# HGRN scores in one product for two heads: each query traded to the other head's tile, the second head read back by a transpose

## The chip, the cores and the metric

The kernel runs on one core of a Trainium2 chip. The metric is the device time of one execution in microseconds (us), as the median of three runs. A profile of one further execution gives the trace that is read here. The engines are called TensorE (PE in the rows; PEld is its loading of stationary operands), VectorE (DVE), ScalarE (ACT), GpSimd (POOL) and SyncE (SP, which issues most transfers).

## What is computed

A trunk of two layers over 256 positions of width 2048, in float32. Layer 0 mixes positions with a gated recurrence (HGRN2, 16 heads of width 128, chunks of 64), layer 1 with a gMLP; each is followed by a squared-ReLU MLP of width 8192. The change lies in the scores of the recurrence alone:

```
b = jnp.cumsum(g_t, axis=2)                                  # log decay, inside a chunk
rel = b[:, :, :, None, :] - b[:, :, None, :, :]
decay = jnp.exp(jnp.where(causal[:, :, None], rel, -jnp.inf))
scores = jnp.einsum('bhtd,bhtsd,bhsd->bhts', q_t, decay, k_t)
o = o_inter + jnp.einsum('bhts,bhse->bhte', scores, v_t)
```

The decay depends on query, key and feature, so the scores are no plain product. The kernel splits the causal triangle of 128 positions into levels. At the level with half-blocks of `h` positions, queries in the second half of a block of `2h` meet keys in its first half; both are scaled by their decay to the boundary between them, and a plain product over features gives the scores of that level. The levels are `h` = 32, 16, 8, the blocks of 8 on the diagonal (scaled to a point inside them), and `h` = 64 (between the two chunks of a 128 block).

## The kernel before

Weights come from HBM in tiles of 1 MB (`raw`, three buffers). Each is split in two: ScalarE casts it to a rounded part (line 127) and VectorE subtracts that for the rest (line 128), so that every projection is a few fast products of rounded operands (lines 158, 160 and 169 to 171). The split tiles `wt` are in a pool of five; a cast has to wait until TensorE has used the tile whose place it takes.

The recurrence runs over eight pairs of heads (`hp`, the loop of line 311). For each pair four projections are made: forget gates, queries, values (for two pairs at once, in even `hp`), gates. Tiles such as `k`, `q`, `dl` and `gl` are 128 features x 2 heads x 256 positions. For `h` = 32, 16, 8, VectorE makes exponents (lines 363, 364), ScalarE their exponential (365), and VectorE multiplies by key in the first halves and by query in the second halves of one tile `gl` (line 370). `kd`, `qd` are the operands of the diagonal blocks, `g64` that of level 64, and `gx` that of the scores between the two blocks of 128.

Line 411 then makes, for each of the five levels, four 128x128 products: two heads times two blocks of 128. In `gl` keys and queries lie side by side, so each product gives keys by queries of one head in the wanted corner, and useless numbers elsewhere. Line 413 copies the wanted places from PSUM into `Pm` under a mask (COPY_PREDICATED), for both heads and blocks in one instruction of 512 columns. Lines 433 and 434 multiply `Pm` by the values into `po`; lines 436 to 442 square and sum that into `pn`; the closure `norm` of line 451 is run in the next pair and fills `S2[hp]` (`s_7` in the rows for the last pair), which the out-projection needs.

These score products, and transposes, take plain float32 operands; the trace has two MATMUL records for such a product (line 411: 5 levels x 4 products x 8 pairs = 160 products, 320 records) and one for a transpose.

The order of instructions on each engine is made by a scheduler that places them on a timeline of its own; `high_priority` and `issue_after` in the code move a few of them. Each engine takes its instructions strictly in that order. Small products share four PSUM banks in turn (`bank`).

Of the kernel before, what the change touches and what calls it, by code (L numbers as in the profile page):

```python
# [8 lines left out]
F32 = mybir.dt.float32  # L9
FR = mybir.dt.float32r  # L10
U8 = mybir.dt.uint8
AF = mybir.ActivationFunctionType
ALU = mybir.AluOpType
PSUM = bass.MemoryType.PSUM

P = 128
T = 256
# [16 lines left out]
def trunk(ctx: ExitStack, tc: tile.TileContext, x, norm_mix, norm_mlp, final_norm, hgrn_w_in, hgrn_w_out,  # L34
# [3 lines left out]
    V, S, G, M = nc.vector, nc.scalar, nc.gpsimd, nc.tensor  # L38

    cp = ctx.enter_context(tc.tile_pool(name="cp", bufs=1))  # L40
# [160 lines left out]
                                       op0=ALU.mult, op1=ALU.subtract)  # L201


    masks = cp.tile([P, 5, P], U8, name="masks")
    rows0 = cp.tile([32, P], F32, name="rows0")
    rows = cp.tile([81, P], F32, name="rows")
    cols0 = cp.tile([P, 32], F32, name="cols0")
# [11 lines left out]
    with tc.tile_pool(name="x0", bufs=1) as x0, tc.tile_pool(name="x1", bufs=2) as x1:  # L219
        xt = [ht[:, :, c * 512:(c + 1) * 512] for c in range(4)]  # L220
        ssp = x0.tile([P, 2, 4], F32, name="ssp")
        nc.scalar.dma_start(out=rows0, in_=norm_mix.rearrange("l (k p) -> (l k) p", p=P))
        raws = [[raw_tile(0, 0), raw_tile(0, 1)],
                [raw_tile(1, 0), x0.tile([P, 8, 256], F32, name="raw1_1")]]
        for c in range(4):
            for h in range(2 if c == 0 else 1):
                w = 256 if c == 0 else 512
                nc.sync.dma_start(out=xt[c][:, :, h * w:(h + 1) * w],
                                  in_=x[0, :, c * 512 + h * w:c * 512 + (h + 1) * w].rearrange("(a p) d -> p a d", p=P))
                if c == 0:  # L230
                    load_part(0, raws[0][0], 2 * h, 2 * h + 2)
            for n in range(2):
                if n or c:
                    load_part(n, raws[n][c // 2], 4 * c, 4 * c + 4)
        pw = [psw.tile([P, 2, 512], F32, tag="pw", name=f"pw{n}") for n in range(2)]
        pc = bank("pc0")
        M.transpose(pc[:, 0:32], rows0, ident[0:32, 0:32])
        V.tensor_copy(cols0, pc[:, 0:32])
        for c in range(4):
            to_features(c, cols0)  # L240
            for n in range(2):
                split_weights(n, raws[n][c // 2], c, parts=1 if c or n else 2)
                mm_feat(pw[n], ready[n], S1, range(4 * c, 4 * c + 4))
        state["load"] = state["use"] = 2
        nc.sync.dma_start(out=rows[0:32, :], in_=norm_mlp.rearrange("l (k p) -> (l k) p", p=P))
        nc.sync.dma_start(out=rows[32:80, :], in_=hgrn_lb_logits.rearrange("l (k p) -> (l k) p", p=P))
        nc.sync.dma_start(out=rows[80:81, :], in_=hgrn_g_norm)
        mf32 = x0.tile([P, 5, P], F32, name="mf32")
        nc.sync.dma_start(out=mf32, in_=level_masks.rearrange("l p t -> p l t"))
        G.tensor_copy(masks, mf32)  # L250
        pc = bank("pc")
        M.transpose(pc[:, 0:81], rows, ident[0:81, 0:81])
        V.tensor_copy(cols, pc[:, 0:81])
        for c in range(4):
            for j in range(2):
                junk = x1.tile([P, 512], F32, tag="junk", name=f"junk{c}{j}")
                if j:
                    V.scalar_tensor_tensor(junk, xt[c][:, j, :], 1.0, xt[c][:, j, :], op0=ALU.mult, op1=ALU.mult,
                                           accum_out=ssp[:, j, c:c + 1])
                else:  # L260
                    S.activation(junk, xt[c][:, j, :], AF.Square, accum_out=ssp[:, j, c:c + 1])
        s2 = x0.tile([P, 2, 2], F32, name="s2")
        V.tensor_tensor(s2, ssp[:, :, 0:2], ssp[:, :, 2:4], op=ALU.add)
        ms = x0.tile([P, 2], F32, name="ms")
        V.tensor_tensor(ms, s2[:, :, 0], s2[:, :, 1], op=ALU.add)
        V.tensor_scalar(ms, ms, 1.0 / D, EPS, op0=ALU.mult, op1=ALU.add)
        G.tensor_tensor(r0c, ms, mhalf[:, 0:2], op=ALU.pow)
# [29 lines left out]
    with tc.tile_pool(name="hg", bufs=1) as hg, tc.tile_pool(name="hg2", bufs=2) as hg2:  # L297
# [1 line left out]
        G.memset(reset, 1.0)  # L299
        G.memset(reset[:, :, 0:1], 0.0)  # L300
        Pm = [hg.tile([P, 2, 3, P], F32, name=f"Pm{i}") for i in range(2)]
        for t in Pm:
            G.memset(t, 0.0)

        def wide(pool, tag, name):
# [2 lines left out]
        def flat(t):  # L308
            return t.rearrange("p a t -> p (a t)")

        for hp in range(NP):
# [41 lines left out]
            V.scalar_tensor_tensor(flat(q), flat(thq), 1.0, flat(zq), op0=ALU.add, op1=ALU.mult)  # L353


            Gs = []
            for h in (32, 16, 8):
                dl = wide(hg2, "dl", f"{hp}_{h}")
# [6 lines left out]
                S.activation(dl, dl, AF.Exp)  # L365
                gl = wide(hg2, "gl", f"{hp}_{h}")
                gv = flat(gl).rearrange("p (b j i) -> p b j i", j=2, i=h)
                for j, src in ((0, k), (1, q)):
                    sv = flat(src).rearrange("p (b j i) -> p b j i", j=2, i=h)
                    V.tensor_tensor(gv[:, :, j, :], dv[:, :, j, :], sv[:, :, j, :], op=ALU.mult)  # L370
                Gs.append((gl, gl))
            dd = wide(hg2, "dl", f"{hp}_d")
            cv = flat(c).rearrange("p (b i) -> p b i", i=8)
            V.tensor_tensor(flat(dd).rearrange("p (b i) -> p b i", i=8), cv,
# [4 lines left out]
            S.activation(kd, dd, AF.Exp, scale=-1.0)  # L379
            V.tensor_tensor(qd, qd, q, op=ALU.mult)  # L380
            V.tensor_tensor(kd, kd, k, op=ALU.mult)
            Gs.append((kd, qd))
            de = wide(hg2, "dl", f"{hp}_e")
            c8 = flat(c).rearrange("p (b i) -> p b i", i=64)
            V.tensor_tensor(flat(de).rearrange("p (b i) -> p b i", i=64), c8[:, :, 63:64].to_broadcast([P, 8, 64]),
# [6 lines left out]
            def ch(t):  # L392
                return t.rearrange("p a (m i) -> p a m i", i=64)

            g64 = wide(hg, "g64", hp)
            V.tensor_tensor(ch(g64)[:, :, 0::2, :], ch(ek)[:, :, 0::2, :], ch(k)[:, :, 0::2, :], op=ALU.mult)
            V.tensor_tensor(ch(g64)[:, :, 1::2, :], ch(eq)[:, :, 1::2, :], ch(q)[:, :, 1::2, :], op=ALU.mult)
            Gs.append((g64, g64))
            gx = wide(hg, "gx", hp)
            V.tensor_tensor(ch(gx)[:, :, 0::3, :], ch(g64)[:, :, 0::3, :],  # L400
                            ch(eq)[:, :, 1:3, 63:64].to_broadcast([P, 2, 2, 64]), op=ALU.mult)
            V.tensor_tensor(ch(gx)[:, :, 1, :], ch(ek)[:, :, 1, :], ch(k)[:, :, 1, :], op=ALU.mult)
            V.tensor_tensor(ch(gx)[:, :, 2, :], ch(eq)[:, :, 2, :], ch(q)[:, :, 2, :], op=ALU.mult)

            pm = Pm[hp % 2]
            for li, (kl, ql) in enumerate(Gs):
                sc = bank(f"sc{hp}_{li}")
                scv = sc.rearrange("p (a b t) -> p a b t", a=2, b=2)
                for j in range(2):
                    for b in range(2):  # L410
                        M.matmul(scv[:, j, b, :], lhsT=kl[:, j, b * P:(b + 1) * P], rhs=ql[:, j, b * P:(b + 1) * P],  # L411
                                 start=True, stop=True)
                V.copy_predicated(pm[:, :, 0::2, :],  # L413
                                  masks[:, li:li + 1, :].unsqueeze(1).to_broadcast([P, 2, 2, P]), scv)
            sx = bank(f"sx{hp}")
            sxv = sx.rearrange("p (a t) -> p a t", a=4)
            for j in range(2):
# [105 lines left out]
    st = Stats("c")  # L523
# [160 lines left out]
def _level_masks():  # L684
    import numpy as np

    s = np.arange(P)[:, None]
    t = np.arange(P)[None, :]
    m = [(s // (2 * h) == t // (2 * h)) & (s % (2 * h) < h) & (t % (2 * h) >= h) for h in (32, 16, 8)]
    m.append((s // 8 == t // 8) & (s <= t))  # L690
    m.append((s < 64) & (t >= 64))
    return np.stack(m).astype(np.float32)


# [19 lines left out]
```

## Time and profile before

| | before |
|---|---|
| median of 3 runs (lowest to highest) | 2217.31 us (2216.74 to 2219.0) |
| the profiled execution | 2219.78 us |
| its span, first to last instruction | 2218.0 us |
| TensorE busy | 2205.0 us, 99% |
| VectorE busy | 1343.0 us, 61% |
| ScalarE busy | 1047.8 us, 47% |
| granted TensorE clock, mean | 0.999 |

A time of the trace is compared with the profiled execution's own span; 1.78 us of that execution lie outside it. The recurrence takes about the first 470 us. In a timeline a row gives the start, the duration, the engine and line, and `x16` for sixteen records merged in one row. Matmuls are pipelined: a row's duration includes the tail that overlaps the next one, so the cost of a product on TensorE is read from start to start. The same holds for VectorE, where an instruction starts shortly before the listed end of the one ahead.

### The profile page before, as it was taken

How to read it: one execution, taken by the hardware profiler on the slowest of the kernel's cores; microseconds unless marked ns; L12 is line 12 of the kernel's file. 1: busy time of each engine (PE TensorE's matmuls, PEld its weight loads, DVE VectorE, ACT ScalarE, POOL GpSimd, SP SyncE). 2: the span in 40 equal slices, each digit the busy share in tenths (PEclk: the TensorE clock that was granted, in tenths of full speed). 3: DMA queues.
4: the chain of work that ended last, by engine and by line, in shares of the span. 5: the costliest groups of instructions: out<-in, count | busy, mean ns of one | idle time of the engine just before them, and what ended most of it. 6: DMA issues, size and time to landing. Idle time of an engine off the chain costs nothing.

```text
span 2218.0 us, 27973 instructions
## 1 busy us (share of the span) xinstructions
PE 2205.0 (99%) x11512; PEld 1894.9 (85%) x11512; DVE 1343.0 (61%) x1593; ACT 1047.8 (47%) x1293; POOL 10.2 (0%) x23
## 2 busy tenths in 40 slices
PE   9999999999999999999999999999999999999998
PEld 7888888888888888888888888888888888888887
DVE  7787877756555555555555558656555545554554
ACT  6666566555434433443444544444434433443443
POOL 0000000000000000000000000000000000000000
PEclk9999999999999999999999999999999999999999
DMA  7555555556556556655655657656566556556653
GB/s 239 166 171 168 157 171 153 191 179 188 192 190 195 193 190 193 191 178 192 202 194 187 205 171 215 206 184 195 185 200 191 193 176 206 191 191 189 191 181 123
DMA packets 309761, 414.28 MB, mean 187 GB/s; under 512 B 6801, under 2 KB 210818, under 8 KB 309378
## 3 DMA queue, kind: packets, MB, share of 16 engines
q1 hardware_dynamic: 309010, 411.44, 58.1%
q8 instruction: 90, 1.47, 0.3%
q10 hardware_dynamic: 624, 1.07, 0.1%
q14 instruction: 37, 0.30, 0.0%
HBM read 410.38 MB, written 2.10 MB: 186 GB/s over the span
## 4 chain that ended last, share of the span: by engine, by line
PE 99%; DMA 0%; issue 0%; ACT 0%; SPq 0%; DVE 0%; POOLq 0%; POOL 0%; ACTq 0%
PE pw L158 32%; PE pw L160 17%; PE pw L169 15%; PE pw L171 15%; PE pw L170 15%; PE sc L411 2%; PE xT L195 1%; DMA raw<-in_hgrn_w_in 0%; PE mix L599 0%; PE po L433 0%; PE pw L640 0%; PE pw L638 0%; PE pw L639 0%; PE pn L442 0%; PE sx L418 0%
## 5 line engine op out<-in xcount | busy, mean ns | idle before, releaser
L128 DVE TENSOR_TENSOR wt<-raw,wt 128x1024 fp32r<-128x1024 f32 (+1 forms) x769 | 923.5, 1220 | 758.1 <-ACT wt L127 757.8
L127 ACT CAST wt<-raw 128x1024 fp32r<-128x1024 f32 (+1 forms) x769 | 789.5, 1049 | 892.1 <-PE pw L171 458.4
L158 PE MATMUL pw<-s,wt 128*128 128x512 f32 x3072 | 733.5, 393 | 3.8 <-ACT wt L127 2.4
L158 PEld LDWEIGHTS pw<-s,wt 128*128 128x128 f32 x3072 | 568.9, 189 | 118.9 <-ACT wt L127 3.1
L169 PE MATMUL pw<-wt,s 128*128 128x512 f32 x1504 | 587.5, 391 | 0.0
L171 PE MATMUL pw<-wt,s 128*128 128x512 f32 x1504 | 587.0, 390 | 0.0
L170 PE MATMUL pw<-wt,s 128*128 128x512 f32 x1504 | 586.5, 390 | 0.0
L160 PEld LDWEIGHTS pw<-s,wt 128*128 128x128 f32 x3072 | 386.3, 191 | 10.9
L160 PE MATMUL pw<-s,wt 128*128 128x256 f32 x3072 | 391.4, 283 | 0.0
L171 PEld LDWEIGHTS pw<-wt,s 128*128 128x128 f32 x1504 | 282.3, 188 | 59.3
L170 PEld LDWEIGHTS pw<-wt,s 128*128 128x128 f32 x1504 | 282.4, 188 | 58.8
L169 PEld LDWEIGHTS pw<-wt,s 128*128 128x128 f32 x1504 | 282.4, 188 | 58.6 <-DVE z_f L179 0.2
L185 ACT CAST s<-a 128x512 fp32r<-128x512 f32 x64 | 39.6, 619 | 136.0 <-DVE a L518 136.0
L186 DVE TENSOR_TENSOR s<-a,s 128x512 fp32r<-128x512 f32 x64 | 44.3, 692 | 37.1 <-ACT s L185 37.1
L518 DVE SCALAR_TENSOR_TENSOR a<-z_ff 128x512 f32<-128x512 f32 x64 | 43.9, 685 | 0.3
L179 DVE TENSOR_TENSOR z_ff<-pw,tb_ff 128x512 f32<-128x512 f32 x64 | 43.8, 684 | 0.0
L178 ACT COPY tb_ff<-pw 128x512 f32<-128x512 f32 x64 | 37.2, 582 | 0.0
L199 ACT ACTIVATE s<-xT,cols 128x256 fp32r<-128x256 f32 x64 | 27.7, 473 | 19.3 <-PE xT L195 12.1
L200 DVE SCALAR_TENSOR_TENSOR s<-xT,cols,s 128x256 fp32r<-128x256 f32 x64 | 28.4, 479 | 8.8 <-ACT s L199 8.6
L413 DVE COPY_PREDICATED Pm<-masks,sc 128x512 f32<-128x512 uint8 x40 | 29.4, 734 | 1.2
L497 DVE SCALAR_TENSOR_TENSOR ht<-pw,col_c,ht 128x512 f32<-128x512 f32 x32 | 22.5, 746 | 5.3 <-PE pw L171 5.3
L411 PEld LDWEIGHTS sc<-gl 128*128 128x128 f32 x192 | 23.5, 191 | 0.8
(189 smaller groups left out, 733.4 us busy)
## 6 DMA issues: line engine op xcount, KB each, us to landing
raw<-in_mlp_w SPq DMA_DIRECT2D x256, 1024.0 KB, 5.7
raw<-in_hgrn_w_in SPq DMA_DIRECT2D x60, 1024.0 KB, 5.8
raw<-in_gmlp_w_in SPq DMA_DIRECT2D x32, 1024.0 KB, 5.6
raw<-in_hgrn_w_out SPq DMA_DIRECT2D x16, 1024.0 KB, 5.1
raw<-in_gmlp_w_out SPq DMA_DIRECT2D x16, 1024.0 KB, 5.1
raw<-in_hgrn_w_in SPq DMA_DIRECT2D x7, 512.0 KB, 9.5
ht<-in_x SPq DMA_DIRECT2D x3, 512.0 KB, 8.7
gb<-in_gmlp_ln_gain SPq DMA_DIRECT2D x8, 128.0 KB, 4.9
```

The source lines that it names most:

```text
L127: S.copy(wt[:, kk, 0:width], src[:, kk, :])
L128: V.tensor_tensor(wt[:, kk, width:2 * width], src[:, kk, :], f32(wt[:, kk, 0:width]), op=ALU.subtract)
L158: M.matmul(pt[:, n, :], lhsT=wt[:, n * P:(n + 1) * P], rhs=xk, start=(k == 0), stop=False)
L160: M.matmul(pt[:, n, 256:512], lhsT=wt[:, 256 + n * P:256 + (n + 1) * P], rhs=xk[:, 0:256], start=False, stop=(k == KT - 1))
L169: M.matmul(pt[:, n, :], lhsT=hi, rhs=wt[:, 0:512], start=(k == 0), stop=False)
L170: M.matmul(pt[:, n, :], lhsT=hi, rhs=wt[:, 512:1024], start=False, stop=False)
L171: M.matmul(pt[:, n, :], lhsT=lo, rhs=wt[:, 0:512], start=False, stop=(k == KT - 1))
L179: V.tensor_tensor(dst, pt[:, :, 0:256], tb, op=ALU.add)
L185: S.copy(dst[:, :, 0:256], src)
L186: V.tensor_tensor(dst[:, :, 256:512], src, f32(dst[:, :, 0:256]), op=ALU.subtract)
L411: M.matmul(scv[:, j, b, :], lhsT=kl[:, j, b * P:(b + 1) * P], rhs=ql[:, j, b * P:(b + 1) * P], start=True, stop=True)
L518: V.scalar_tensor_tensor(a.rearrange("p a t -> p (a t)"), z.rearrange("p a t -> p (a t)"), 0.0, z.rearrange("p a t -> p (a t)"), op0=ALU.m ...
```

## The change

Queries trade heads. In `gl` and `g64`, head 0's tile keeps its own keys but gets the queries of head 1, and the other way round. One product of tile 0 (stationary) by tile 1 (moving) then has, where the row is a key place and the column a query place, the scores of head 0, and where the row is a query place and the column a key place, the scores of head 1, transposed. So levels 32, 16, 8 and 64 take two products (one for each block of 128) and not four. Their result goes through a new tile `Px` under masks of both corners, in copies of 256 columns. What lies above the diagonal blocks in `Px` is copied to head 0's part of `Pm` under a sixth mask; TensorE transposes `Px` (two transposes into bank `st`), and VectorE copies the same places of that to head 1's part. The diagonal level keeps its four products (`sd`).

For each pair this makes 12 score products and 2 transposes of what was 20 products. On VectorE, multiplications by queries become two smaller ones (one for each head), the part of `gx` that reads `g64` becomes three, and five masked copies of 512 columns become one of 512 and six of 256: 24 instructions for 16. The masks are 6 x 128 columns for 5 x 128, their transfer 384 KB for 320 KB.

```diff
-                for j, src in ((0, k), (1, q)):
-                    sv = flat(src).rearrange("p (b j i) -> p b j i", j=2, i=h)
-                    V.tensor_tensor(gv[:, :, j, :], dv[:, :, j, :], sv[:, :, j, :], op=ALU.mult)
-                Gs.append((gl, gl))
+                kv = flat(k).rearrange("p (b j i) -> p b j i", j=2, i=h)
+                V.tensor_tensor(gv[:, :, 0, :], dv[:, :, 0, :], kv[:, :, 0, :], op=ALU.mult)
+                for a in range(2):
+                    V.tensor_tensor(second(gl[:, 1 - a, :], h), second(dl[:, a, :], h), second(q[:, a, :], h), op=ALU.mult)
+                Gs.append(gl)
...
-            V.tensor_tensor(ch(g64)[:, :, 1::2, :], ch(eq)[:, :, 1::2, :], ch(q)[:, :, 1::2, :], op=ALU.mult)
-            Gs.append((g64, g64))
+            for a in range(2):
+                V.tensor_tensor(ch(g64)[:, 1 - a, 1::2, :], ch(eq)[:, a, 1::2, :], ch(q)[:, a, 1::2, :], op=ALU.mult)
+            Gs.append(g64)
             gx = wide(hg, "gx", hp)
-            V.tensor_tensor(ch(gx)[:, :, 0::3, :], ch(g64)[:, :, 0::3, :],
-                            ch(eq)[:, :, 1:3, 63:64].to_broadcast([P, 2, 2, 64]), op=ALU.mult)
+            V.tensor_tensor(ch(gx)[:, :, 0, :], ch(g64)[:, :, 0, :],
+                            ch(eq)[:, :, 1, 63:64].to_broadcast([P, 2, 64]), op=ALU.mult)
+            for a in range(2):
+                V.tensor_scalar(ch(gx)[:, a, 3, :], ch(g64)[:, 1 - a, 3, :], ch(eq)[:, a, 2, 63:64], None, op0=ALU.mult)
...
-            for li, (kl, ql) in enumerate(Gs):
+            px = Px[hp % 2]
+            for li, gl in zip((0, 1, 2, 4), Gs):
                 sc = bank(f"sc{hp}_{li}")
-                scv = sc.rearrange("p (a b t) -> p a b t", a=2, b=2)
-                for j in range(2):
-                    for b in range(2):
-                        M.matmul(scv[:, j, b, :], lhsT=kl[:, j, b * P:(b + 1) * P], rhs=ql[:, j, b * P:(b + 1) * P],
-                                 start=True, stop=True)
-                V.copy_predicated(pm[:, :, 0::2, :],
-                                  masks[:, li:li + 1, :].unsqueeze(1).to_broadcast([P, 2, 2, P]), scv)
+                for b in range(2):
+                    M.matmul(sc[:, b * P:(b + 1) * P], lhsT=gl[:, 0, b * P:(b + 1) * P], rhs=gl[:, 1, b * P:(b + 1) * P],
+                             start=True, stop=True)
+                V.copy_predicated(px, masks[:, li:li + 1, :].to_broadcast([P, 2, P]),
+                                  sc[:, 0:T].rearrange("p (b t) -> p b t", b=2))
+            sc = bank(f"sd{hp}")
+            scv = sc.rearrange("p (a b t) -> p a b t", a=2, b=2)
+            for j in range(2):
+                for b in range(2):
+                    M.matmul(scv[:, j, b, :], lhsT=kd[:, j, b * P:(b + 1) * P], rhs=qd[:, j, b * P:(b + 1) * P],
+                             start=True, stop=True)
+            V.copy_predicated(pm[:, :, 0::2, :], masks[:, 3:4, :].unsqueeze(1).to_broadcast([P, 2, 2, P]), scv)
+            apart = masks[:, 5:6, :].to_broadcast([P, 2, P])
+            V.copy_predicated(pm[:, 0, 0::2, :], apart, px)
+            st = bank(f"st{hp}")
+            for b in range(2):
+                M.transpose(st[:, b * P:(b + 1) * P], px[:, b, :], ident)
+            V.copy_predicated(pm[:, 1, 0::2, :], apart, st[:, 0:T].rearrange("p (b t) -> p b t", b=2))
```

Three places show how the order moves. In these rows a name ends in a number of its own; the lines of the changed kernel are 418 (score products), 426 (diagonal products), 433 (transposes), 438 (`sx`) and 453, 454 (`po`), and 420, 428, 430, 434 (masked copies). The first place is TensorE in the first pair, from the score products to `po`; before:

```order
162 L411 MATMUL sc_2_567<-gl_8_531 128x128 x4
163 L411 MATMUL sc_3_573<-qd_536,kd_537 128x128 x4
164 L411 MATMUL sc_4_579<-g_0_548 128x128 x4
165 L418 MATMUL sx_585<-gx_551 128x128 x2
166 L158 MATMUL pw_734<-s_2_91,wt_1_594 128x512 x2
167 L158 MATMUL pw_734<-s_3_92,wt_1_594 128x512 x4
168 L160 MATMUL pw_734<-s_0_89,wt_0_591 128x256 x4
169 L160 MATMUL pw_734<-s_1_90,wt_0_591 128x256 x4
170 L160 MATMUL pw_734<-s_2_91,wt_1_594 128x256 x4
171 L160 MATMUL pw_734<-s_3_92,wt_1_594 128x256 x3
172 L433 MATMUL po_705<-Pm_439,v_702 128x256
```

The same stretch of TensorE in the changed kernel, in two parts, the first from level 64 to the transposes:

```order
167 L418 MATMUL sc_4_577<-g_0_555 128x128 x2
168 L426 MATMUL sd_581<-qd_543,kd_544 128x128 x4
169 L160 MATMUL pw_741<-s_1_90,wt_0_598 128x256 x3
170 L160 MATMUL pw_741<-s_2_91,wt_1_601 128x256 x4
171 L160 MATMUL pw_741<-s_3_92,wt_1_601 128x256 x4
172 L158 MATMUL pw_741<-s_4_93,wt_2_606 128x512 x4
173 L158 MATMUL pw_741<-s_5_94,wt_2_606 128x512
174 L433 MATMUL st_588<-ident,Px_441 128x128 x2
```

and the second from there to `po`:

```order
175 L438 MATMUL sx_592<-gx_559 128x128 x2
176 L158 MATMUL pw_741<-s_5_94,wt_2_606 128x512 x3
177 L158 MATMUL pw_741<-s_6_95,wt_3_609 128x512 x4
178 L158 MATMUL pw_741<-s_7_96,wt_3_609 128x512 x4
179 L160 MATMUL pw_741<-s_4_93,wt_2_606 128x256 x4
180 L160 MATMUL pw_741<-s_5_94,wt_2_606 128x256 x4
181 L160 MATMUL pw_741<-s_6_95,wt_3_609 128x256 x2
182 L453 MATMUL po_712<-Pm_439,v_709 128x256
```

Where one group of 14 products stood and then `po`, there are now a group of level 64 and the diagonal, 16 products of the gate projection, the transposes with `sx`, and 21 more products of that projection ahead of `po`.

The second place is VectorE at the same point of the first pair, where the copies stand among the weight subtractions of line 128; before:

```order
91 L400 TENSOR_TENSOR gx_551<-g_0_548,e_eq_546 128x2x2x64
92 L128 TENSOR_TENSOR wt_0_720<-raw_0_718,wt_0_720 128x4x256
93 L413 COPY_PREDICATED Pm_439<-masks,sc_2_567 128x2x2x128
94 L413 COPY_PREDICATED Pm_439<-masks,sc_3_573 128x2x2x128
95 L413 COPY_PREDICATED Pm_439<-masks,sc_4_579 128x2x2x128
96 L128 TENSOR_TENSOR wt_1_723<-raw_0_718,wt_1_723 128x4x256
```

and in the changed kernel:

```order
96 L428 COPY_PREDICATED Pm_439<-masks,sd_581 128x2x2x128
97 L430 COPY_PREDICATED Pm_439<-masks,Px_441 128x2x128
98 L128 TENSOR_TENSOR wt_1_730<-raw_0_725,wt_1_730 128x4x256
99 L128 TENSOR_TENSOR wt_2_735<-raw_1_733,wt_2_735 128x4x256
100 L434 COPY_PREDICATED Pm_439<-masks,st_588 128x2x128
```

The copy that `po` needs last is now that of the transposes, and it stands behind two weight subtractions (one in odd pairs) that it did not stand behind.

The third place is TensorE at the end of the recurrence, where the out-projection first needs `S2[7]` (`s_7` here); before:

```order
1056 L170 MATMUL pw_4067<-wt_5_3903,s_5_102 128x512
1057 L171 MATMUL pw_4067<-wt_5_3903,s_5_102 128x512
1058 L169 MATMUL pw_3914<-wt_7_3789,s_7_104 128x512
1059 L170 MATMUL pw_3914<-wt_7_3789,s_7_104 128x512
1060 L169 MATMUL pw_4067<-wt_5_3903,s_5_102 128x512
```

and in the changed kernel:

```order
1098 L170 MATMUL pw_4095<-wt_6_3936,s_6_103 128x512
1099 L171 MATMUL pw_4095<-wt_6_3936,s_6_103 128x512
1100 L169 MATMUL pw_3942<-wt_7_3817,s_7_104 128x512
1101 L170 MATMUL pw_3942<-wt_7_3817,s_7_104 128x512
1102 L169 MATMUL pw_4095<-wt_7_3939,s_7_104 128x512
```

Between the second `pn` product of the last pair and the first use of `s_7` stood 43 products of the out-projection, and stand 30 now. After the first out-projection column the two orders agree but for the numbers of names and lines.

## Rows read from the trace of the kernel before

**Rows 1.** The page: busy time of each engine, and the chain's shares by engine.

```profile
PE 2205.0 (99%) x11512; PEld 1894.9 (85%) x11512; DVE 1343.0 (61%) x1593; ACT 1047.8 (47%) x1293; POOL 10.2 (0%) x23
...
PE 99%; DMA 0%; issue 0%; ACT 0%; SPq 0%; DVE 0%; POOLq 0%; POOL 0%; ACTq 0%
```

**Rows 2.** Waits of TensorE, whole span: us in total, times, longest.

```profile
PE pw L158 <- ACT wt L127: 2.4, 1, 2.4
PE pw L158 <- DVE s L200: 1.4, 1, 1.4
PE wps L212 <- POOL mhalf L59: 1.1, 1, 1.1
```

**Rows 3.** Busy time by stretch: window, sum, engines, granted clock, DMA share, GB/s.

```profile
50.00:470.00 420.00, 420.00 (x2380) 368.66 (x2379) 324.96 (x471) 254.80 (x339) 0.00 (x0) 1.00 0.55 167
```

**Rows 4.** Timeline of TensorE, first pair: start, duration, instruction, records merged.

```profile
65.84 1.05 PE L411 MATMUL sc<-gl 128*128 128x128 f32 x8
66.72 1.06 PE L411 MATMUL sc<-qd,kd 128*128 128x128 f32 x8
...
68.51 0.61 PE L418 MATMUL sx<-gx 128*128 128x128 f32 x4
68.88 1.62 PE L158 MATMUL pw<-s,wt 128*128 128x512 f32 x6
70.33 1.96 PE L160 MATMUL pw<-s,wt 128*128 128x256 f32 x15
72.13 0.60 PE L433 MATMUL po<-Pm,v 128*128 128x256 f32 x2
...
73.56 3.81 PE L158 MATMUL pw<-s,wt 128*128 128x512 f32 x16
77.21 1.59 PE L160 MATMUL pw<-s,wt 128*128 128x256 f32 x12
```

**Rows 5.** Timeline of TensorE at transposes in the out-projection.

```profile
468.57 0.38 PE L195 MATMUL xT<-ident,ht 128*128 128x128 f32 x2
468.71 0.48 PE L171 MATMUL pw<-wt,s 128*128 128x512 f32 x1
469.02 0.82 PE L195 MATMUL xT<-ident,ht 128*128 128x128 f32 x6
469.59 0.48 PE L169 MATMUL pw<-wt,s 128*128 128x512 f32 x1
469.91 0.40 PE L170 MATMUL pw<-wt,s 128*128 128x512 f32 x1
```

**Rows 6.** Groups by line and shape, first 560 us: busy, mean ns, idle before.

```profile
L195 PE MATMUL xT<-ident,ht 128*128 128x128 f32 x64 | 11.2, 310 | 0.0
L127 ACT CAST wt<-raw 128x1024 fp32r<-128x1024 f32 x180 | 186.1, 1048 | 120.7 <-PE pw L160 66.5 <-PE pw L171 41.1 <-DMA raw<-in_mlp_w 5.7
```

**Rows 7.** Timeline of VectorE, first pair.

```profile
64.14 1.22 DVE L128 TENSOR_TENSOR wt<-raw,wt 128x1024 fp32r<-128x1024 f32 x1
65.27 0.75 DVE L413 COPY_PREDICATED Pm<-masks,sc 128x512 f32<-128x512 uint8 x1
65.89 0.42 DVE L396 TENSOR_TENSOR g<-l_ek,k 128x256 f32<-128x256 f32 x1
66.22 0.30 DVE L402 TENSOR_TENSOR gx<-l_ek,k 128x128 f32<-128x128 f32 x1
66.42 0.43 DVE L400 TENSOR_TENSOR gx<-g,e_eq 128x256 f32<-128x256 f32 x1
```

**Rows 8.** Waits of VectorE for casts, first 560 us: total, times, longest.

```profile
DVE wt L128 <- ACT wt L127: 104.2, 65, 4.4
```

**Rows 9.** Timelines of TensorE and ScalarE at the end of the last pair.

```profile
449.97 0.40 PE L442 MATMUL pn<-o2s,onesr 128*128 128x512 f32 x1
...
450.99 1.04 ACT L127 CAST wt<-raw 128x1024 fp32r<-128x1024 f32 x1
...
455.52 0.62 ACT L185 CAST s<-kd_on 128x512 fp32r<-128x512 f32 x1 [0.60 <-DVE kd_on L458]
```

**Rows 10.** Transfers: KB each, us from issue to landing.

```profile
mf<-level_masks SPq DMA_DIRECT2D x1, 320.0 KB, 6.2
```

More of the change, by code (lines that the diff above doesn't have):

```diff
@@ L201, in to_features @@
                                        op0=ALU.mult, op1=ALU.subtract)
-    masks = cp.tile([P, 5, P], U8, name="masks")
+    masks = cp.tile([P, 6, P], U8, name="masks")
     rows0 = cp.tile([32, P], F32, name="rows0")
@@ L247, in trunk @@
         nc.sync.dma_start(out=rows[80:81, :], in_=hgrn_g_norm)
-        mf32 = x0.tile([P, 5, P], F32, name="mf32")
+        mf32 = x0.tile([P, 6, P], F32, name="mf32")
         nc.sync.dma_start(out=mf32, in_=level_masks.rearrange("l p t -> p l t"))
@@ L301, in trunk @@
         Pm = [hg.tile([P, 2, 3, P], F32, name=f"Pm{i}") for i in range(2)]
-        for t in Pm:
+        Px = [hg.tile([P, 2, P], F32, name=f"Px{i}") for i in range(2)]
+        for t in Pm + Px:
             G.memset(t, 0.0)
@@ L353, in trunk, with second @@
             V.scalar_tensor_tensor(flat(q), flat(thq), 1.0, flat(zq), op0=ALU.add, op1=ALU.mult)
+            def second(t, h):
+                return t.rearrange("p (b j i) -> p b j i", j=2, i=h)[:, :, 1, :]
             Gs = []
@@ L381, in trunk @@
             V.tensor_tensor(kd, kd, k, op=ALU.mult)
-            Gs.append((kd, qd))
             de = wide(hg2, "dl", f"{hp}_e")
@@ L688, in _level_masks @@
     t = np.arange(P)[None, :]
-    m = [(s // (2 * h) == t // (2 * h)) & (s % (2 * h) < h) & (t % (2 * h) >= h) for h in (32, 16, 8)]
+    m = [(s // (2 * h) == t // (2 * h)) & (s // h != t // h) for h in (32, 16, 8)]
     m.append((s // 8 == t // 8) & (s <= t))
-    m.append((s < 64) & (t >= 64))
+    m.append(s // 64 != t // 64)
+    m.append(s // 8 < t // 8)
     return np.stack(m).astype(np.float32)
```

## The prediction

> **What bounds the kernel now.** I read the page's first part, then the waits of TensorE, then the busy time of the stretch that the change touches. TensorE is busy 99% of the span, and the chain of work that ended last is TensorE for 99% of it [rows 1]. In the whole span it waits three times, 4.9 us together [rows 2], and none of these waits is a wait for a score or a copy. From 50 to 470 us, which holds the recurrence from the first score on, TensorE is busy for all 420 us, at a granted clock of 1.00, while VectorE is busy for 325 us, so idle for 95, and ScalarE for 255 [rows 3]. So a product that is taken from TensorE's queue there shortens the span by what it occupies, unless the changed order makes TensorE wait where it did not. VectorE counts only through such waits.
>
> **Removed: 64 score products.** Per pair 20 products become 12: eight fewer, 64 in eight pairs. Their price is read from start to start. The group of 14 products in the first pair starts at 65.84, the products of line 158 behind it at 68.88, and those six end at 70.33 [rows 4]. A product of line 158 in steady flow takes (77.21 − 73.56) / 16 = 0.228 us [rows 4], so the 14 cost 70.33 − 65.84 − 6 × 0.228 = 3.12 us, or 0.223 each, the loss at the change of kind included. The lower bound is the same group without what follows it, (68.88 − 65.84) / 14 = 0.217: the six products behind it take 1.45 us, 0.09 more than six in steady flow, and a removed product inside a group need not bring its share of that. I take 0.223, with which every other group of rows 4 comes out too (four products from 65.84 to 66.72 are 0.88, against 0.89): 64 × 0.223 = 14.3 us; at 0.217 it is 13.9.
>
> **Added: 16 transposes.** Two a pair. At 468.57 two transposes, a fast product, six transposes and another fast product pass by 469.91 [rows 5]: 1.34 us, less two fast products at 0.228, for eight transposes, 0.11 each. Upper bound: they overlap with nothing, at the 310 ns that one of them lasts [rows 6]. Lower bound: nothing, if they hide in the group of `sx` that they precede, against which the row speaks. 16 × 0.11 = 1.8 us, between 0 and 5.0. On this the Trainium skill (page "TensorE: Matmul & The Clock Gate", section "Part 4: PE-mode transpose") says that a 128x128 transpose took about 275 ns in one kernel, and that the full clock does not engage for transposes. By that figure the sixteen cost 4.4 us, and the change would leave 2207.4 us (an estimate). Rows 5 disagree on the price, and rows 3 give a clock of 1.00 over a stretch that ends on these transposes.
>
> **Added: changes of kind.** The score products of a pair stand in more and smaller groups: seven more changes from plain float32 back to fast products, net, in the new order. The price 0.223 already carries one for 14 products; another costs between nothing and the 0.09 above, so 0 to 0.6 us. I take 0, because the transposes' groups of two and six cost the same per piece.
>
> **VectorE.** By starts [rows 7]: 0.33 us for 256 columns, 0.20 for 128, 0.62 for a masked copy of 512. A copy of 256 has no row; it lies between 0.33 and 0.62, and I take 0.35, by the multiplication of the same size, which is the nearest row. Per pair before: six and two multiplications at 0.33, `gx` at 0.33 + 2 × 0.20, five copies at 0.62: 6.5 us. After: 3 × (0.33 + 0.40), 0.33 + 0.40, `gx` at most 5 × 0.20, 0.62 + 6 × 0.35: 6.6 us. So 0.2 us more a pair, 1.8 if small copies cost as much as large ones: 1 to 15 us in all, within the 95 idle us of rows 3. I cost it at nothing; what it costs if that cover fails is the second rival.
>
> **The new link.** `po` now waits for scores, copy, transposes, second copy. First pair, even-numbered: from the end of level 64 to the transposes TensorE has the four diagonal products (0.89), 11 products of line 160 at 0.12 (15 from 70.33 to 72.13 [rows 4]) and 5 of line 158, together 3.35 us; VectorE needs one copy, at most 0.62. Then from the transposes to `po` lie `sx` (0.45), 11 products of line 158 (2.5) and 10 of line 160 (1.2): 4.15 us. Ahead of the last copy stand two weight subtractions (1.13 each [rows 7]), whose casts (1.05 [rows 6]) wait for tiles that TensorE gives back 8 products of line 160 and 5 of line 158 before the transposes, 2.1 us, and right ahead of those. Two casts, a subtraction and a copy are 3.85 us from the first release, so the copy ends 3.85 − 2.1 − 0.22 = 1.5 us behind the transposes, 2.6 us early. Odd pairs have one subtraction and some 3.6 us of products, 3 us early by the same count. Cost: nothing.
>
> **Ends and queues.** At the end of the last pair TensorE reaches `s_7` after 30 products (6.8 us) and not 43. Before, the second `pn` product started at 449.97 and `s_7` was cast by 455.52 + 0.62 [rows 9], 6.2 us later, with a weight cast (1.04) between that no longer stands there: 0.6 to 1.7 us early, cost nothing, at worst a few tenths, once. The longer mask transfer is 64 KB more on SP's queue ahead of the value weights: 320 KB took 6.2 us [rows 10], so 1.2 us at most, while the casts behind wait for TensorE far longer than for transfers [rows 6]: nothing. GpSimd's larger cast and two more fills lie beside this.
>
> **Sum.** 14.3 − 1.8 = 12.5 us. The profiled span goes from 2218.0 to 2205.5, its execution from 2219.78 to 2207.3; that execution is 2.5 above the median of the runs, so the median goes from 2217.31 to 2204.8. With the bounds: 13.9 − 5.0 − 0.6 = 8.3 us saved (2209.0) to 14.3 (2203.0).
>
> **Rivals.** What a measurement here can tell from no change is about 0.2%, 4.4 us.
> (a) Transposes at their full duration: 310 ns each [rows 6], 5.0 us: 9.3 saved, 2208.0. The mechanism is that lone transposes do not overlap with what surrounds them. Rows 5 speak against it, but they hold one group of two only. Chance 0.06. The 275 ns of the Trainium skill's page above would act in the same way.
> (b) The link comes late, and the kernel gets slower: the copy of the transposes stands behind the subtractions, and they behind casts. VectorE waits for casts 65 times in the first 560 us, 104.2 us in total, 1.6 on average, 4.4 at the longest [rows 8]. With the average twice ahead of each copy, an even pair loses 3.2 − 2.6 = 0.6 us, four of them 2.4: 2207. With the longest wait twice in even and once in odd pairs, 4 × 6.2 + 4 × 1.4 = 30 us: 2235. It decides from waits of 3.4 us each on: then four even pairs lose 4.2 each, 17 us, and the kernel is at 2221.8, over 0.2% slower. Against it speaks that the tiles come free ahead of the transposes. Slower: 0.04; a middle of it, with 8 to 17 us given back (2213 to 2222), 0.05.
> (c) It does not do what it says: half the products at the traded levels do not take half the time, since their groups shrink from four or eight to two. If the 64 that stay there cost 0.36 each and not 0.223, 9 of the 12.5 us are gone: 2214. Against it: in rows 5 two transposes cost no more per piece than six. Chance 0.03.
>
> **How the numbers follow.** The forecast with its own bounds has 0.82. With (a), faster is 0.88; (c) and the middle of (b) make the same 0.08; slower 0.04. The range takes the bounds 2203.0 and 2209.0, and around them how far the runs shown lie from their median (0.6 below, 1.7 above): 2202.4 to 2210.7. It holds the forecast and (a), and leaves out (b) and (c).
>
> **What would show it.** Right: in the changed profile TensorE has 112 records fewer (128 less 16) and still waits only in the first 12 us; its busy time is some 12 us lower; transposes of `Px` start 0.11 us apart; VectorE's busy time moves by under 14 us. Wrong: a wait of TensorE for a copy of line 430 or 434 or for `s_7`, more of VectorE's waits for casts next to line 434, or a start-to-start price of the small groups above 0.25 us a product.

## The result: 1.0% slower, and the time was lost in instructions that the change does not touch

| | before | after |
|---|---|---|
| median (lowest to highest) | 2218.15 us (2216.74 to 2219.28, 4 runs) | 2240.13 us (2239.19 to 2240.52, 4 runs) |
| the profiled execution, its span | 2219.78, 2218.0 us | 2239.9, 2238.1 us |
| granted TensorE clock, mean | 0.999 | 0.997 |

The ratio is 1.0098, with a 95% interval of 1.0086 to 1.0110. Forecast were 2204.8 us, in a range of 2202.4 to 2210.7: the sign was wrong, and the size by 35 us.

The page of after, its busy times and the chain's shares (compare [rows 1]):

```profile
PE 2224.0 (99%) x11400; PEld 1881.9 (84%) x11400; DVE 1343.5 (60%) x1657; ACT 1048.2 (47%) x1293; POOL 10.8 (0%) x25
...
PE 99%; DMA 0%; issue 0%; ACT 0%; SPq 0%; DVE 0%; POOLq 0%; POOL 0%; ACTq 0%
```

All that TensorE waits for in after, with total, times and longest in us (compare [rows 2]):

```profile
PE pw L158 <- ACT wt L127: 2.6, 1, 2.6
PE pw L158 <- DVE s L200: 1.8, 1, 1.8
PE wps L212 <- POOL mhalf L59: 1.1, 1, 1.1
PE xT L195 <- DMA ht<-in_x: 0.4, 1, 0.4
```

TensorE has the 112 records fewer that the change promises, still bounds the kernel, and waits hardly longer than before: 5.9 us against 4.9, and for no copy and no `s_7`. Yet it is busy for 2224.0 us, against 2205.0. So it did not wait longer; it took longer for less work.

Where? The transposes of line 195 mark the same points of the program in both kernels, up to a different order in the first column of the out-projection: the first group after the recurrence, the one before the gMLP, and the one before the second MLP. Timeline of TensorE at the second and third of these points, before (the first is at 468.57 [rows 5]):

```profile
1162.38 0.38 PE L195 MATMUL xT<-ident,ht 128*128 128x128 f32 x2
...
1438.92 0.38 PE L195 MATMUL xT<-ident,ht 128*128 128x128 f32 x2
```

and at all three after:

```profile
461.42 0.49 PE L195 MATMUL xT<-ident,ht 128*128 128x128 f32 x3
...
1165.42 0.38 PE L195 MATMUL xT<-ident,ht 128*128 128x128 f32 x2
...
1446.68 0.38 PE L195 MATMUL xT<-ident,ht 128*128 128x128 f32 x2
```

The recurrence, the only stretch that was edited, is left 7.15 us earlier. Everything behind it does the same work, and is slower: from the first mark to the second 704.00 us for 693.81, to the third 281.26 for 276.54, to the end 791.4 for 779.1. That is 10.2 + 4.7 + 12.3 = 27.2 us lost, and 27.2 − 7.15 gives the 20.1 us between the spans.

It is not the clock. Busy time by stretch, inside the first of these stretches (window, sum, engines with records, granted clock, DMA share, GB/s), before:

```profile
530.00:1150.00 620.00, 620.00 (x3192) 531.35 (x3192) 344.03 (x347) 262.00 (x290) 0.00 (x0) 1.00 0.60 194
```

and after:

```profile
530.00:1150.00 620.00, 620.00 (x3144) 523.81 (x3143) 339.38 (x342) 257.77 (x285) 0.00 (x0) 1.00 0.59 190
```

In 620 us at a clock of 1.00, without a wait in either, TensorE gets through 48 records fewer. Groups by line (busy us, mean ns of one, idle before), before:

```profile
L158 PE MATMUL pw<-s,wt 128*128 128x512 f32 x3072 | 733.5, 393 | 3.8 <-ACT wt L127 2.4 <-DVE s L200 1.4
L169 PE MATMUL pw<-wt,s 128*128 128x512 f32 x1504 | 587.5, 391 | 0.0
```

and after:

```profile
L158 PE MATMUL pw<-s,wt 128*128 128x512 f32 x3072 | 741.1, 395 | 4.4 <-ACT wt L127 2.6 <-DVE s L200 1.8
L169 PE MATMUL pw<-wt,s 128*128 128x512 f32 x1504 | 594.4, 395 | 0.0
```

The fast products of 512 columns, the same 3072 of line 158 and 1504 each of lines 169, 170 and 171, are busy for longer. Their price is read from start to start. In the first MLP 32 products of line 158 stand in one row, with the next row's start behind them; before:

```profile
561.22 7.49 PE L158 MATMUL pw<-s,wt 128*128 128x512 f32 x32
568.54 3.98 PE L160 MATMUL pw<-s,wt 128*128 128x256 f32 x32
572.36 7.49 PE L158 MATMUL pw<-s,wt 128*128 128x512 f32 x32
```

and after:

```profile
565.81 7.59 PE L158 MATMUL pw<-s,wt 128*128 128x512 f32 x32
573.24 4.00 PE L160 MATMUL pw<-s,wt 128*128 128x256 f32 x32
577.07 7.59 PE L158 MATMUL pw<-s,wt 128*128 128x512 f32 x32
```

Before, 32 take 568.54 − 561.22 = 7.32 us; after, 573.24 − 565.81 = 7.43. The 256-column products of line 160 hardly differ, 3.82 and 3.83. Products of lines 169 to 171 in a row, before and then after, nine steps apart in each:

```profile
639.74 0.39 PE L171 MATMUL pw<-wt,s 128*128 128x512 f32 x1
...
641.78 0.39 PE L171 MATMUL pw<-wt,s 128*128 128x512 f32 x1
```

```profile
599.83 0.40 PE L170 MATMUL pw<-wt,s 128*128 128x512 f32 x1
...
601.92 0.40 PE L170 MATMUL pw<-wt,s 128*128 128x512 f32 x1
```

2.04 us for nine steps, then 2.09: 227 and 232 ns. Averaged over all such steps under 300 ns (some 60 longer ones in each trace left out), line 158 goes from 228.7 to 232.4 ns and lines 169 to 171 from 227.4 to 232.6: 3072 × 3.7 + 4512 × 5.2 ns = 34.8 us. Less the 12.5 us forecast as saved this makes 22.3, and 22.0 were measured. The whole miss is the price of products that the change does not touch. The steps also have a pattern, which the trace gives in ns; groups of 96 products of lines 169 to 171 (in the MLPs, one column of 512 with its eight weight tiles), medians of six groups, for the first three weight tiles and for the fourth:

```
before  tiles 1 to 3:  227 227 227 227 227 227      tile 4:  234 224 238 229 237 229 238 229
after   tiles 1 to 3:  238 229 238 229 237 229      tile 4:  232 232 231 227 226 227 227 226
```

Before and after have traded places, and tiles 5 to 8 go with the first three. The fourth tile of each column is the one that comes from a pool of its own in the MLPs (`wtx`); in line 158, whose columns have four weight tiles, it is one in four. So a fast product has two prices here, and what sets them goes with the weight tile's pool.

### The profile page after: what moved, and what is told of

It is laid out like the page before. It is cut to its first block, busy times and chain, and to the rows that moved or that the text cites. A ratio compares the mean times of both kernels' runs of the same rounds, so it can differ in the third digit from the quotient of the medians.

```text
span 2238.1 us, 27791 instructions
## 1 busy us (share of the span) xinstructions
PE 2224.0 (99%) x11400; PEld 1881.9 (84%) x11400; DVE 1343.5 (60%) x1657; ACT 1048.2 (47%) x1293; POOL 10.8 (0%) x25
## 4 chain that ended last, share of the span: by engine, by line
PE 99%; DMA 0%; issue 0%; ACT 0%; SPq 0%; DVE 0%; POOLq 0%; POOL 0%; ACTq 0%
PE pw L158 32%; PE pw L160 16%; PE pw L169 16%; PE pw L171 16%; PE pw L170 16%; PE sc L418 1%; PE xT L195 1%; DMA raw<-in_hgrn_w_in 0%; PE sd L426 0%; PE mix L619 0%; PE po L453 0%; PE pw L660 0%; PE pw L658 0%; PE pw L659 0%; PE pn L462 0%
## 5 line engine op out<-in xcount | busy, mean ns | idle before, releaser
L158 PE MATMUL pw<-s,wt 128*128 128x512 f32 x3072 | 741.1, 395 | 4.4 <-ACT wt L127 2.6
L169 PE MATMUL pw<-wt,s 128*128 128x512 f32 x1504 | 594.4, 395 | 0.0
L171 PE MATMUL pw<-wt,s 128*128 128x512 f32 x1504 | 594.2, 395 | 0.0
L170 PE MATMUL pw<-wt,s 128*128 128x512 f32 x1504 | 593.6, 395 | 0.0
L517 DVE SCALAR_TENSOR_TENSOR ht<-pw,col_e,ht 128x512 f32<-128x512 f32 x30 | 21.1, 746 | 5.5 <-PE pw L171 5.5
L195 PE MATMUL xT<-ident,ht 128*128 128x128 f32 x128 | 19.3, 282 | 0.4 <-DMA ht<-in_x 0.4
```

The lines of the kernel that those rows point to most:

```text
L158: M.matmul(pt[:, n, :], lhsT=wt[:, n * P:(n + 1) * P], rhs=xk, start=(k == 0), stop=False)
L169: M.matmul(pt[:, n, :], lhsT=hi, rhs=wt[:, 0:512], start=(k == 0), stop=False)
L170: M.matmul(pt[:, n, :], lhsT=hi, rhs=wt[:, 512:1024], start=False, stop=False)
L171: M.matmul(pt[:, n, :], lhsT=lo, rhs=wt[:, 0:512], start=False, stop=(k == KT - 1))
L195: M.transpose(pt[:, k * T + j * P:k * T + (j + 1) * P], ht[:, j, o:o + P], ident)
L517: V.scalar_tensor_tensor(hs, pt[:, j, :], 1.0 if col is None else col[:, j:j + 1], hs, op0=ALU.mult, op1=ALU.add)
```

## The theory, and how it was tested

The change makes the mask tile 6 × 128 bytes of each partition for 5 × 128. The pools of raw and split weight tiles are allocated behind it, so every weight tile lies 128 bytes higher; the activations `s` (`S1`, `S2`) lie ahead of it and stay. Call distance the byte address of a weight tile less that of an activation tile, modulo 256. Inside a tile, operands stand at multiples of 512 bytes, so one number holds for a whole tile. From the allocation of the kernels as built, the five weight tiles of the main pool are at distance 0 from the activations before and 128 after; the two of `wtx` at 128 before and 0 after. That is the exchange which the steps show.

**Theory:** the place of the weight tiles sets the price of the fast products, and nothing else of the change costs time. **Its rival:** the changed work or its order makes them dearer, through more traffic of VectorE or another phase between the engines, and a larger mask tile alone does nothing. Where the expectations of e1 to e4 speak of two theories, they are these. In f1 and f2 the letters A and B stand for two forms of the first.

### e1: the kernel before, with only the larger mask tile

```diff
-    masks = cp.tile([P, 5, P], U8, name="masks")
+    masks = cp.tile([P, 6, P], U8, name="masks")[:, 0:5, :]
```

> The kernel before, with nothing changed but the mask tile, which is made 6 x 128 bytes for 5 x 128 and of which five are used; so every tile that is allocated behind it, the split weights among them, lies 128 bytes higher, and all work and its order stay. Theory A (the place of the weight tiles in SBUF sets the price of a fast product, 227 ns start to start where they lay, 229 to 238 in turn where they lie now): about 2252 us, that is 2218 and the 34 us by which the changed kernel missed 2205.6. Rival B (the changed order and the smaller groups make the fast products slower): 2218 us, no change, and 227 ns.

Measured: 2251.73 us, ratio 1.0146 (1.0131 to 1.0161). No instruction is added, and the kernel loses 33 us. Timeline of TensorE of e1 in the first MLP:

```profile
565.36 7.59 PE L158 MATMUL pw<-s,wt 128*128 128x512 f32 x32
572.79 4.00 PE L160 MATMUL pw<-s,wt 128*128 128x256 f32 x32
```

7.43 us for 32, as in after. The rival falls.

### e2: the changed kernel, with the weight tiles 256 bytes above their old place

```diff
-    masks = cp.tile([P, 6, P], U8, name="masks")
+    masks = cp.tile([P, 7, P], U8, name="masks")[:, 0:6, :]
```

> The changed kernel, with one more row of 128 bytes in the mask tile, unused: the weight tiles then lie 256 bytes higher than in the kernel before and not 128. Theory A, if places repeat every 256 bytes: the fast products are back at 227 ns, and the change shows its own worth, 12.5 us: 2205.6 us. Theory A, if they repeat only every 512 bytes: 2240 us or another time above 2210. Rival B: 2240 us, as the changed kernel.

Measured: 2204.94 us, ratio 0.9936 (0.9922 to 0.9951). The page of e2 and its marks on TensorE's timeline:

```profile
PE 2192.1 (99%) x11400; PEld 1882.1 (85%) x11400; DVE 1343.2 (61%) x1657; ACT 1048.8 (48%) x1293; POOL 10.8 (0%) x25
```

```profile
456.73 0.49 PE L195 MATMUL xT<-ident,ht 128*128 128x128 f32 x3
...
1149.56 0.38 PE L195 MATMUL xT<-ident,ht 128*128 128x128 f32 x2
...
1426.10 0.38 PE L195 MATMUL xT<-ident,ht 128*128 128x128 f32 x2
```

The recurrence ends 11.8 us before that of before, and from the second mark on the stretches last what they last in before (276.54 us, and 779.1 to the end at 2205.2). TensorE's busy time is 12.9 us lower, the span 12.8, the median 13.7. The other 1.0 us lies in the first stretch (692.83 us for 693.81), in whose first column the order differs. So the change itself is worth what was forecast, and a shift of 256 bytes leaves the steps where they were (table below). The changed kernel less e2, the same work with the weight tiles moved, is 2240.13 − 2204.94 = 35.2 us; the steps gave 34.8.

### e3 and e4: the extra pool at distance 0 too

`R1` is allocated ahead of the pool `wtx`, behind the main pool; 32 columns more move `wtx`, and what else lies behind `R1`, by 128 bytes. e3 adds this to e2, e4 makes only this edit in the kernel before.

```diff
-    R1 = late.tile([P, T], F32, name="R1")
+    R1 = late.tile([P, T + 32], F32, name="R1")[:, 0:T]
```

> As the kernel with the weight tiles 256 bytes higher, and one later tile (R1) larger by 128 bytes as well, so that the two extra weight tiles which the MLPs use for the fourth quarter of the weights also lie at the same place within 256 bytes as the others. Theory A: in the kernel before these extra tiles are the slow ones (the fourth of eight tiles at 229 to 238 ns), which costs about 50 ns a projection of 32 products and 86 ns a column of 96, together some 5 us: about 2200.6 us. Rival B: 2240 us.

> The kernel before, with R1 alone larger by 128 bytes, so that only the two extra weight tiles of the MLPs move. Theory A: about 5 us faster, 2213 us, with 227 ns in the fourth quarter of the weights too. Rival B: 2218 us.

Measured: e3 2200.95 us, ratio 0.9919 (0.9903 to 0.9936); e4 2213.66 us, ratio 0.9978 (0.9969 to 0.9988). Timeline of TensorE of e3:

```profile
568.06 7.44 PE L158 MATMUL pw<-s,wt 128*128 128x512 f32 x32
575.34 4.00 PE L160 MATMUL pw<-s,wt 128*128 128x256 f32 x32
```

7.28 us for 32, the least so far: before loses 5 us (2218.6 less e4's 2213.66) to its own `wtx` tiles. With every tile at distance 0 in both, the change is worth 2213.66 − 2200.95 = 12.7 us.

### f1 and f2: the place itself, or the distance from the activations?

A small constant that is allocated ahead of the activations (`mone`) is made 128 bytes wider. In f1 activations and weights move together by 128 bytes; in f2 the larger mask tile of e1 is added, so that the weights move by 256 and the activations by 128.

```diff
-    mone = cp.tile([P, 4], F32, name="mone")
+    mone = cp.tile([P, 36], F32, name="mone")[:, 0:4]
```

> The kernel before with a small constant that is made first 128 bytes wider, so that the activation tiles and all weight tiles lie 128 bytes higher, and their distances from each other are as in before. Theory A (the place of the weight tiles within 256 bytes alone sets the price of a fast product): 2252 us, as e1, and fast products of line 158 start 232 to 233 ns apart. Theory B (what counts is the distance of the weight tiles from the activation tiles, within 256 bytes): 2218.5 us, as before, 227 ns apart.

> The kernel before with that constant 128 bytes wider and the mask tile 128 bytes wider too: the activation tiles lie 128 bytes higher, the weight tiles 256 bytes higher, which is the same place within 256 bytes as in before. Theory A (place of the weight tiles alone): 2218.5 us, 227 ns. Theory B (distance of weight tiles from activation tiles): 2252 us, 232 to 233 ns, as e1.

Measured: f1 2217.98 us, ratio 1.0 (0.999 to 1.001); f2 2254.03 us, ratio 1.0156 (1.0141 to 1.0171). TensorE's timelines, of f1 and then of f2:

```profile
569.80 7.49 PE L158 MATMUL pw<-s,wt 128*128 128x512 f32 x32
577.12 3.98 PE L160 MATMUL pw<-s,wt 128*128 128x256 f32 x32
```

```profile
569.14 7.59 PE L158 MATMUL pw<-s,wt 128*128 128x512 f32 x32
576.57 4.00 PE L160 MATMUL pw<-s,wt 128*128 128x256 f32 x32
```

7.32 and 7.43 us. Weight tiles at e1's place cost nothing in f1, and weight tiles at before's place (modulo 256) cost as much as e1's in f2. Form A falls: it is the distance between the two operands. The raw tiles moved with the main pool in both, so what ScalarE and VectorE read and write there kept its distances, and traffic between those does not explain f2.

### f3 and f4: distances of 64 and 32 bytes

`warm`, one column wide, lies between activations and weights; 16 columns more move the weights by 64 bytes (f3), 8 by 32 (f4).

```diff
-    warm = cp.tile([P, 1], F32, name="warm")
+    warm = cp.tile([P, 17], F32, name="warm")[:, 0:1]
```

> The kernel before with the weight tiles 64 bytes higher, the activation tiles where they were. If there are only two prices, one for tiles at the old place within 128 bytes and one beside it: 2218.5 or 2252 us. If the price grows with the distance from the old place up to 128 bytes: about 2235 us, 230 ns from one product of line 158 to the next.

> The kernel before with the weight tiles 32 bytes higher, the activation tiles where they were. If there are only two prices: 2218.5 or 2252 us. If the price grows with the distance from the old place: about 2227 us, 228 to 229 ns from one product of line 158 to the next.

Measured: f3 2228.69 us, ratio 1.0047 (1.0032 to 1.0062); f4 2255.48 us, ratio 1.0166 (1.0151 to 1.0181). Both expectations missed: there are more than two prices, and they do not grow with the distance. Timeline of TensorE of f3:

```profile
561.62 7.59 PE L158 MATMUL pw<-s,wt 128*128 128x512 f32 x32
569.05 3.93 PE L160 MATMUL pw<-s,wt 128*128 128x256 f32 x32
572.83 7.59 PE L158 MATMUL pw<-s,wt 128*128 128x512 f32 x32
```

In f3 line 158 pays as much as in e1 (7.43 us), but line 160 pays less than before (572.83 − 569.05 = 3.78), and so do lines 169 to 171 against e1, as the table shows. The steps of f3 in ns say why these lines differ from line 158 (medians; main pool at distance 64, `wtx` at 192):

```
line 158         distance 64:  231 236 231 236 231 236      distance 192:  229 232 226 229 232 226
lines 169 to 171 distance 64:  226 229 232 226 229 232      distance 192:  236 231 236 231 236 231
```

Line 158 holds the weights and streams the activations; lines 169 to 171 hold the activations and stream the weights. What 64 does to one, 192 (64 the other way round) does to the other: the price goes with the address of the streamed operand less that of the held one.

All runs but the last two, with the mean step from one product to the next of the same kind (ns, from the trace; steps over 300 ns, in line 160 over 250, left out):

| run | distance, main pool / `wtx` | line 158 | lines 169 to 171 | line 160 | median, us |
|---|---|---|---|---|---|
| before | 0 / 128 | 228.7 | 227.4 | 119.6 | 2217.3 to 2218.6 |
| after | 128 / 0 | 232.4 | 232.6 | 120.0 | 2240.13 |
| e1 | 128 / 0 | 232.3 | 232.6 | 119.6 | 2251.73 |
| e2 | 0 / 128 | 228.7 | 227.4 | 119.9 | 2204.94 |
| e3 | 0 / 0 | 227.9 | 226.9 | 120.2 | 2200.95 |
| e4 | 0 / 0 | 227.9 | 226.9 | 119.9 | 2213.66 |
| f1 | 0 / 128 | 228.6 | 227.5 | 119.6 | 2217.98 |
| f2 | 128 / 0 | 232.3 | 232.6 | 119.7 | 2254.03 |
| f3 | 64 / 192 | 232.6 | 229.3 | 117.0 | 2228.69 |
| f4 | 32 / 160 | 233.2 | 233.2 | 118.9 | 2255.48 |

### g1 and g2: distance 0 for the wide products, another for line 160

Line 160 holds the rest parts of the 256-column weight tiles. Its price was lowest in f3, so g1 takes e3 and puts only those rest parts 64 bytes off, g2 192 bytes off; the tiles are 64 elements longer for it, and the products of the last columns read the rest parts at their new place. The core of g1 (in g2 1072 and 2096):

```diff
-        wt = pool.tile([P, 2048], FR, tag=tag, name=f"wt{n}_{q}").rearrange("p (k n) -> p k n", k=kw)
+        wt = pool.tile([P, 2112], FR, tag=tag, name=f"wt{n}_{q}")
+        if width == 256:
+            hi = wt[:, 0:1024].rearrange("p (k n) -> p k n", k=kw)
+            lo = wt[:, 1040:2064].rearrange("p (k n) -> p k n", k=kw)
...
```

> e3 with the rest parts of the 256-column weight tiles (stationary in the 256-column products of line 160) 64 bytes off the place of the activations, and all else at distance 0. In f3 a weight tile 64 bytes higher gave 113 ns from one such product to the next in the recurrence and 118 ns in the MLPs, where before and e3 have 120. If that comes from the distance of the rest parts themselves: about 3,250 products 2 to 7 ns shorter, 6 to 23 us less than e3, 2178 to 2195 us. If it needs the products of line 158 ahead of them at that distance too: 2201 us, as e3.

> As g1, with the rest parts 192 bytes off. If the sign of the distance counts for 256-column products, this differs from g1; if those products take 120 ns again: 2201 us, as e3. The last eight products of each group of 32 in f3, whose weight tiles lay 192 bytes off, took 118 ns: by that 2195 us.

Measured: g1 2195.66 us, ratio 0.9898 (0.9882 to 0.9913); g2 2196.85 us, ratio 0.9902 (0.9884 to 0.992). Timeline of TensorE of g1, whose lines 164 and 166 are 158 and 160:

```profile
567.38 7.44 PE L164 MATMUL pw<-s,wt 128*128 128x512 f32 x32
574.66 3.93 PE L166 MATMUL pw<-s,wt 128*128 128x256 f32 x32
578.43 7.44 PE L164 MATMUL pw<-s,wt 128*128 128x512 f32 x32
```

32 products of line 166 take 3.77 us, against 3.83 in after; the mean step is 118.3 ns for e3's 120.2, and 3072 × 1.9 ns = 5.8 us, against 5.3 between the medians. That is just short of the 6 to 23 us that were expected: most steps of f3 in the recurrence took 113 or 114 ns, and few of g1's did. In g2 the mean step is 118.4 ns, so for these products 64 and 192 bytes come out alike. g1 is the quickest version here, 22.7 us under the kernel before; the intervals of g1, g2 and e3 overlap, so their order is less certain than that each beats both kernels.

## Why the prediction was wrong, point by point

**What bounds the kernel** was right: TensorE at 99%, with no wait for a score or a copy.

**The terms of the sum were right.** Timeline of TensorE in the first pair of after (lines 418 and 426 are the score products, 433 the transposes, 453 `po`):

```profile
58.97 1.05 PE L418 MATMUL sc<-gl 128*128 128x128 f32 x8
59.78 0.48 PE L171 MATMUL pw<-wt,s 128*128 128x512 f32 x1
60.10 0.39 PE L169 MATMUL pw<-wt,s 128*128 128x512 f32 x1
...
70.77 0.38 PE L433 MATMUL st<-ident,Px 128*128 128x128 f32 x2
70.99 0.61 PE L438 MATMUL sx<-gx 128*128 128x128 f32 x4
...
75.17 0.59 PE L453 MATMUL po<-Pm,v 128*128 128x256 f32 x2
```

Four score products take 0.81 us, and the fast product behind them 0.32 instead of 0.23, so 0.90 or 0.225 each: forecast were 0.223. (By its own rows the prediction's loss at a change of kind is 1.45 − 6 × 0.228 = 0.08 us, not 0.09; nothing hangs on it.) Two transposes take 0.22, forecast 0.11 each. With the wide products at before's price, e2 shows 12.8 us less span and e3 against e4 12.7 us less time, for 12.5 forecast. On the transposes the Trainium skill (page "TensorE: Matmul & The Clock Gate", section "Part 4: PE-mode transpose") has about 275 ns, by which the change would have been worth 9.9 us (an estimate). The 0.22 us for two speak against that price here; 272 ns is what the record of one transpose lasts at the median in the trace of before, the overlapped tail included.

**VectorE and the new link** were right, and cost nothing. Timeline of VectorE in the first pair of after:

```profile
63.10 0.45 DVE L420 COPY_PREDICATED Px<-masks,sc 128x256 f32<-128x256 uint8 x1
63.44 1.21 DVE L128 TENSOR_TENSOR wt<-raw,wt 128x1024 fp32r<-128x1024 f32 x1
...
69.93 2.36 DVE L128 TENSOR_TENSOR wt<-raw,wt 128x1024 fp32r<-128x1024 f32 x2 [0.21 <-ACT wt L127]
72.20 0.44 DVE L434 COPY_PREDICATED Pm<-masks,st 128x256 f32<-128x256 uint8 x1
```

A masked copy of 256 columns takes 0.34 us, forecast 0.35; VectorE's busy time rises by 0.5 us, less than the 1 to 15 bounded. The last copy stands behind two weight subtractions, as read from the order, and ends at 72.64, 2.5 us before `po`: forecast were 2.6. In the second pair it ends 2.8 us early, forecast 3. Timelines of VectorE and TensorE there:

```profile
133.87 0.45 DVE L434 COPY_PREDICATED Pm<-masks,st 128x256 f32<-128x256 uint8 x1
```

```profile
137.12 0.59 PE L453 MATMUL po<-Pm,v 128*128 128x256 f32 x2
```

**The end of the recurrence** was right: no wait for `s_7`.

**The step that failed** is the last of the part on ends and queues, on the masks. It costed the sixth mask as a transfer ("64 KB more on SP's queue") and as work beside other work ("GpSimd's larger cast and two more fills lie beside this"), and came to nothing. It never asked what stands behind the tile in memory. Those 128 bytes of each partition moved every weight tile against the activations, and e1 shows that this alone costs 33 us, more than twice what the change saves.

Behind it lies a silent one. The 0.228 us of a fast product in steady flow [rows 4] was used to cost what was removed, and taken as a constant for the 7584 wide products that stay. The trace of before spoke against a constant: in the MLPs one weight tile in four of line 158, and one in eight of lines 169 to 171, ran at 232 to 233 ns on average, next to others at 227. A mean over a stretch hides this; steps listed by tile show it.

**The rivals** did not occur. (a) The transposes took 0.11 us. (b) The link came 2.5 us early; the time given for this case, up to 2235, is near the result by chance, since no wait stands behind it. (c) Half the products took half the time. The forecast listed waits and the price of the small groups as what would prove it wrong, and neither did: the price of the large groups was not on the list. One of its signs of being right did fail: TensorE's busy time was to fall by some 12 us, and rose by 19.0.

**What stays open.** The runs show that the price depends on the distance of the two operands modulo 256, with 0 the cheapest of those tried for 512 columns, and that it is not the place of either alone. Why is not shown. That the loading of the next held operand (PEld) and the streaming of the moving one read the same memory at the same time, and meet more often at some distances, would fit, but it is only argued. The records of the loads do not settle it: those of lines 169 to 171 last 188 ns on average both before and after, those of line 160 191 ns before and 188 in f3. Nor is it shown why line 160 prefers another distance, nor why most of its steps took 113 or 114 ns in the recurrence of f3 and 117 or 118 in g1.

## What to carry to other kernels

A tile that grows moves all that is allocated behind it. When an edit changes the size of a small tile, compare the addresses of TensorE's operands before and after, or pad the tile so that what stands behind stays put; here 128 bytes of padding turned 22 us lost into 13 us won. And when a result misses, first compare a stretch of the program that was not edited: if that has moved without a wait and at the same clock, look for a cause outside the work that was changed.

## What was not expected of the hardware

- In wide products (512 columns) at a granted clock of 1.00, the step is 226 to 227 ns at distance 0. At 128 it is 232 to 233 on average (in most of lines 169 to 171 229 and 238 in turn), at 64 or 192 it is 231 and 236 in turn, or 226, 229 and 232. On 7584 products a move from 0 to 128 (and of `wtx` the other way) costs 33 us (e1), 1.5% of the kernel.
- A shift by 256 bytes changes nothing (e2, the one such shift tried), and the pattern turns round with the roles of the operands: 64 for weights held is what 192 is for weights streamed (f3).
- Products of 256 columns took 120 ns at distance 0, and 118 with the held operand 64 or 192 bytes off (g1, g2).
